# Attention in a two-layer trunk: values stationary on two column tiles, probabilities divided before their transposes

## The chip, the core and the metric

The kernel runs on one core of one Trainium2 chip. The metric is the device time of one execution in microseconds (us). The engines of a core are TensorE (PE, matmuls and transposes; its weight loads are shown as PEld), VectorE (DVE), ScalarE (ACT), GpSimd (POOL) and SyncE (SP, which issues DMAs). Each engine takes its instructions in the order in which the program lists them and waits on semaphores for what the others make. SBUF is the memory on the core, PSUM the one that PE writes.

## The reference

A trunk of two layers on 256 tokens of 1024 channels in float32. Each layer projects the tokens to queries, keys, values (8 heads of 64 channels), a recurrent input and a gate. Attention is causal over three patterns of window and dilation; with the bias table built at the start, the three merge into one softmax per head with a bias by distance:

```
s = (q / 8) k^T + bias            # per head, 256 x 256, causal
p = exp(s - max),  Z = sum(p)     # per head and token
O = (p v) / Z                     # 256 tokens x 512 channels
y = [rms_norm(O) * g_attn, rms_norm(gelu(gate) * h) * g_lru]     # h: linear recurrence
x = layer_norm(alpha x + y W_out)
```

Then comes a feed-forward part: a dense SwiGLU in layer 0, eight SwiGLU experts of which each token takes two in layer 1. RMS norm divides by the root of the mean square over all 512 channels of a token.

## The kernel before

All work is written out in program order, and each engine runs its list from first to last. Products in float32 are made from splits: a matrix is written as a high part (`hi`, by ACT) and the rest (`lo`, by DVE, as the difference), and three matmuls hi*hi, hi*lo, lo*hi replace one. Weights come in units of 1 MB through a stream of buffers (`WeightStream`): a DMA is issued when a buffer becomes free, which is when the split that reads it is done. `U.ahead(n)` puts the splits of the next units into the lists of ACT and DVE at that place. The list of what may be loaded ends early until the router has told which experts come (`U.open`); after that the expert stage streams all remaining weights. Experts with at most 64 tokens work on unsplit weights in two column tiles: 64 stationary columns go to output partitions 0 to 63, 64 others to 64 to 127.

In a mixer the order around the change is this. PE projects keys, gate and values. Scores get bias and maximum on DVE, and ACT takes the exponentials into `P0[par]` (queries 0 to 127: 128 tokens x 4 heads x 128 keys) and `P1[par]` (queries 128 to 255, 256 keys), one pair for the even heads and one for the odd, with the sums in `Z` (token x half x head). After the projection of the values (`vt`) PE transposes the probabilities (L719 to L723), four 128x128 blocks at a time: eight blocks of each parity into a PSUM buffer `big`, four into a buffer `sm`. ACT copies the eight to `PTa` (L724), DVE the four to `PTb` (L725). There are two `big` buffers, and the next user of both is the recurrent branch's part of the output product. ACT then squares the branch's result `gt` (L726), POOL adds the squares over the four channel blocks (L727, L728), and the output product of the recurrent branch runs on PE in two calls of `out_l` of 24 matmuls each. Between the two stand the sum of the squares over the partitions by a matmul with ones (`pss`), from which DVE and POOL make the factor `rl` (L361, L362), and probabilities times values: 8 matmuls for the first 128 queries, 16 for the others, with the transposed probabilities as stationary and 64 channels of one head as moving operand. The result has tokens on partitions. DVE multiplies it by 1/Z (L777), ACT squares and sums it (L778), DVE and POOL make `ra`, PE transposes it in blocks (L785, four inside the second `out_l`, four behind), and ACT and DVE split the transposes into `Ah` and `Al` (L792, L794). With these runs the attention part of the output product, 48 matmuls, whose results are added to the residual with the factor `ra` (L820).

The listing gives the code with its line numbers; in the profile nearly all matmuls carry L245, the line of the helper.

Of the kernel before, what the change touches and what calls it, by code (L numbers as in the profile page):

```python
# [9 lines left out]
F32 = mybir.dt.float32  # L10
F32R = mybir.dt.float32r
I32 = mybir.dt.int32
AF = mybir.ActivationFunctionType
ALU = mybir.AluOpType
AX = mybir.AxisListType

P = 128
D = 1024
S = 256
H = 8  # L20
DA = 512
# [7 lines left out]
RMS_EPS = 1e-6  # L29
# [174 lines left out]
def trunk(ctx, tc, x, xT, w_in, w_out, prm, wbd, rb, ohc, cst, ln1_g, ln1_b, ln2_g, ln2_b,  # L204
          ffn_w_gate, ffn_w_up, ffn_w_down, router_w, moe_w_gate, moe_w_up, moe_w_down, out):
    nc = tc.nc
    V, A, T, G = nc.vector, nc.scalar, nc.tensor, nc.gpsimd
# [8 lines left out]
    def sm(shape=None):  # L216
        cnt[0] += 1
        t = ps.tile([P, 512], F32, name=f"sm{cnt[0]}", tag="sm", bufs=4)
        if shape:
            t = t.rearrange("p (a b) -> p a b", a=shape)  # L220
        return t
# [22 lines left out]
    def mm(o, l, r, first, last):  # L244
        T.matmul(o, l, r, start=first, stop=last)  # L245

    units = []
    TS = [slice(0, P), slice(P, S)]
# [79 lines left out]
    ident = csts[:, 0:128]  # L328
# [12 lines left out]
    ones = base.tile([P, 2], F32, name="ones")  # L341
# [18 lines left out]
    def rsqrt(o, ms, eps, scale):  # L360
        V.tensor_scalar(o, ms, scale, eps, op0=ALU.mult, op1=ALU.add)  # L361
        G.tensor_tensor(out=o, in0=o, in1=mhalf, op=ALU.pow)  # L362
# [194 lines left out]
    def mixer(L, pool, prev):  # L557
        def mt(shape, name, dt=F32):
            if name in SLOT:
                return pool.tile(shape, dt, name=f"{name}_{L}", tag=f"m4_{SLOT[name]}")  # L560
            m2 = math.prod(shape[1:]) == 512
            if m2:
                return pool.tile(shape, dt, name=f"{name}_{L}", tag="m2", bufs=NM2)
            return lnp.tile(shape, dt, name=f"{name}_{L}", tag=name)
# [22 lines left out]
        if prev is None:  # L587
            banks()
            p = big(2)
# [29 lines left out]
        for g, (dst, bi) in enumerate(((rg, 5), (ig, 6))):  # L619
            p = big(4)  # L620
# [31 lines left out]
        P0 = [mt([P, 4, P], f"P0{par}") for par in range(2)]  # L652
# [59 lines left out]
        PTb = [mt([P, 4, P], f"PTb{par}") for par in range(2)]  # L712
        A.activation(Lh, gt, AF.Copy)
        V.tensor_tensor(out=Ll, in0=gt, in1=Lh.bitcast(F32), op=ALU.subtract)
        for par in range(2):
            pa = big(8)
            pb = sm(4)
            for c in range(4):
                T.transpose(pa[:, c, :], P0[par][:, c, :], ident)  # L719
            for c in range(4):  # L720
                T.transpose(pa[:, 4 + c, :], P1[par][:, c, 0:P], ident)
            for c in range(4):
                T.transpose(pb[:, c, :], P1[par][:, c, P:S], ident)  # L723
            A.activation(PTa[par].rearrange("p j c q -> p (j c) q"), pa, AF.Copy)  # L724
            V.tensor_copy(PTb[par], pb)  # L725
        A.activation(tg, gt, AF.Square)  # L726
        G.tensor_tensor(out=tg[:, 0:2], in0=tg[:, 0:2], in1=tg[:, 2:4], op=ALU.add)  # L727
        G.tensor_tensor(out=tg[:, 0], in0=tg[:, 0], in1=tg[:, 1], op=ALU.add)  # L728
        V.reciprocal(Z, Z)

        r = [ax[:, t, :] for t in range(2)]

# [2 lines left out]
        def out_l(u, mid=None):  # L735
            wh, wl = U.next(2)
            for t in range(2):
                if t and mid:
                    mid()
                if u == 0:  # L740
                    pl[t] = big(2)
                p = pl[t]
                for j in range(2):
                    c = 2 * u + j
                    down_mm((p[:, 0, :], p[:, 1, :]), c == 0, c == 3, Lh[:, c, TS[t]], Ll[:, c, TS[t]],
                            wh[:, j, :], wl[:, j, :])

        def out_r(t):
            V.scalar_tensor_tensor(r[t], pl[t].rearrange("p a b -> p (a b)"), rl[:, t:t + 1], r[t],
                                   op0=ALU.mult, op1=ALU.add)  # L750
# [10 lines left out]
        U.ahead(4)  # L761
        Ah = mt([P, 4, S], "Ah", F32R)
        Al = mt([P, 4, S], "Al", F32R)
        O = mt([P, 2, H, 64], "O")
        Of = [O[:, t].rearrange("p h c -> p (h c)") for t in range(2)]
        for t in range(2):
            sq = mt([P, DA], f"sq{t}")
            p = sm(8)
            for h in range(H):
                par, c = h % 2, h // 2  # L770
                hv = slice(h * 64, (h + 1) * 64)
                if t == 0:
                    mm(p[:, h, :], PTa[par][:, 0, c, :], vt[:, 0, hv], True, True)
                else:
                    mm(p[:, h, :], PTa[par][:, 1, c, :], vt[:, 0, hv], True, False)
                    mm(p[:, h, :], PTb[par][:, c, :], vt[:, 1, hv], False, True)
            V.tensor_tensor(out=O[:, t], in0=p, in1=Z[:, t, :, None].to_broadcast([P, H, 64]), op=ALU.mult)  # L777
            A.activation(sq, Of[t], AF.Square, accum_out=ra[:, t:t + 1])  # L778
            rsqrt(ra[:, t:t + 1], ra[:, t:t + 1], RMS_EPS, 1.0 / DA)
        oT = []  # L780

        def o_transposes(t):
            q = sm(4)
            for c in range(4):
                T.transpose(q[:, c, :], Of[t][:, c * P:(c + 1) * P], ident)  # L785
            oT.append(q)

        out_l(1, lambda: o_transposes(0))
        o_transposes(1)
        for t in range(2):  # L790
            q = oT[t]
            A.activation(Ah[:, :, TS[t]], q, AF.Copy)  # L792
            out_r(t)
            V.tensor_tensor(out=Al[:, :, TS[t]], in0=q, in1=Ah[:, :, TS[t]].bitcast(F32), op=ALU.subtract)  # L794

        if L < DEPTH - 1:
            U._lo(G)
# [692 lines left out]
```

## Time and profile before

| | us |
|---|---|
| median of 3 runs (1257.7 to 1260.06) | 1258.46 |
| the profiled execution | 1258.07 |
| its span, first to last instruction | 1256.2 |
| PE busy in the span | 1214.9 (97%) |
| DVE busy | 650.0 (52%) |
| ACT busy | 518.1 (41%) |
| POOL busy | 81.7 (7%) |
| mean DMA rate | 341 GB/s |

Times in the rows are microseconds from the span's start. A row of a timeline gives the start, the duration from the start of the first to the end of the last of its instructions, the engine, the line, the operation, output and inputs by name (buffer numbers left out), partitions x elements, the count, and in brackets how long the engine stood idle before and what released it. Layer 0's mixer comes first (the rows of it lie between 74 and 96 us), then the dense part (its splits L833 run from 127.1 to 286.9), then layer 1's mixer (its rows lie between 365 and 386 us), the router, and the expert stage, which takes the rest.

### The profile page before, as it was taken

How to read it: one execution, taken by the hardware profiler on the slowest of the kernel's cores; microseconds unless marked ns; L12 is line 12 of the kernel's file. 1: busy time of each engine (PE TensorE's matmuls, PEld its weight loads, DVE VectorE, ACT ScalarE, POOL GpSimd, SP SyncE). 2: the span in 40 equal slices, each digit the busy share in tenths (PEclk: the TensorE clock that was granted, in tenths of full speed). 3: DMA queues.
4: the chain of work that ended last, by engine and by line, in shares of the span. 5: the costliest groups of instructions: out<-in, count | busy, mean ns of one | idle time of the engine just before them, and what ended most of it. 6: DMA issues, size and time to landing. Idle time of an engine off the chain costs nothing. (4 is left out here: it accounts for less than half of the span.)

```text
span 1256.2 us, 18532 instructions
## 1 busy us (share of the span) xinstructions
PE 1214.9 (97%) x7562; PEld 908.3 (72%) x7562; DVE 650.0 (52%) x611; ACT 518.1 (41%) x549; POOL 81.7 (7%) x75
## 2 busy tenths in 40 slices
PE   9999999999999989999999999999999999999884
PEld 8989999998988766666655678875568887565441
DVE  6698544457698964544310398841069883101004
ACT  5784533343782742444210377731057772000001
POOL 3224000004014010000000000000000000000001
PEclk9999999999999999999999999999999999999998
DMA  9853545553468959999999999999999999999993
GB/s 348 317 194 137 200 193 202 201 193 145 158 247 348 373 230 369 420 421 420 421 419 420 420 421 421 421 420 420 421 420 421 421 421 418 421 420 420 421 418 144
DMA packets 63506, 428.99 MB, mean 341 GB/s; under 512 B 7951, under 2 KB 8376, under 8 KB 12984
## 3 DMA queue, kind: packets, MB, share of 16 engines
q1 hardware_dynamic: 62408, 423.55, 83.0%
q0 software_dynamic: 720, 3.68, 0.8%
q8 instruction: 61, 1.00, 0.3%
q10 hardware_dynamic: 288, 0.52, 0.1%
q14 instruction: 29, 0.24, 0.1%
HBM read 426.67 MB, written 2.63 MB: 342 GB/s over the span
## 5 line engine op out<-in xcount | busy, mean ns | idle before, releaser
L148 DVE TENSOR_TENSOR lo<-w,hi 128x2048 fp32r<-128x2048 f32 (+1 forms) x181 | 402.8, 2242 | 79.9 <-ACT hi L130 78.2
L130 ACT ACTIVATE hi<-w 128x2048 fp32r<-128x2048 f32 (+1 forms) x183 | 340.7, 1875 | 88.2 <-PE sm L245 43.9
L245 PE MATMUL sm<-w,g 128*64 128x256 f32 x2240 | 260.9, 382 | 1.4 <-DMA w<-in_moe_w_up_dram 0.9
L245 PEld LDWEIGHTS sm<-w,g 128*64 128x64 f32 x2240 | 157.7, 137 | 95.3 <-issue 23.7
L245 PE MATMUL sm<-hi,g 128*128 128x512 f32 x672 | 220.3, 399 | 0.1
L1280 DVE TENSOR_TENSOR h<-h,sm 128x256 f32<-128x256 f32 (+1 forms) x56 | 29.0, 518 | 273.9 <-PE sm L245 273.9
L1176 ACT ACTIVATE ht<-sm 128x256 f32<-128x256 f32 (+1 forms) x56 | 25.6, 457 | 311.5 <-PE sm L1174 311.5
L245 PEld LDWEIGHTS sm<-hi,g 128*128 128x128 f32 x672 | 126.2, 188 | 32.1 <-issue 2.4
L245 PE MATMUL acc<-w,ht 128*64 128x512 f32 x560 | 135.0, 602 | 10.4 <-DMA w<-in_moe_w_down_dram 9.9
L245 PE MATMUL sm<-lo,g 128*128 128x512 f32 x336 | 133.1, 396 | 1.9 <-DVE lo L148 1.9
L245 PE MATMUL sm<-xh,hi 128*128 128x256 f32 x528 | 132.4, 284 | 0.0
L245 PE MATMUL sm<-xl,hi 128*128 128x256 f32 x528 | 131.9, 283 | 0.0
L245 PE MATMUL acc<-hi,ht 128*128 128x512 f32 x336 | 111.5, 403 | 0.0
L245 PEld LDWEIGHTS sm<-xh,hi 128*128 128x128 f32 x528 | 99.8, 189 | 1.7 <-issue 1.3
L245 PEld LDWEIGHTS acc<-w,ht 128*64 128x64 f32 x560 | 40.3, 138 | 83.4 <-issue 67.6
L245 PEld LDWEIGHTS sm<-xl,hi 128*128 128x128 f32 x528 | 99.6, 189 | 0.4
L245 PE MATMUL sm<-xh,lo 128*128 128x256 f32 x528 | 84.8, 283 | 0.0
L245 PEld LDWEIGHTS acc<-hi,ht 128*128 128x128 f32 x336 | 64.3, 191 | 17.5 <-issue 2.7
L245 PE MATMUL acc<-lo,ht 128*128 128x512 f32 x168 | 68.1, 406 | 8.6 <-DVE lo L148 8.6
L245 PEld LDWEIGHTS sm<-lo,g 128*128 128x128 f32 x336 | 63.2, 188 | 16.8 <-DVE lo L148 2.9
L245 PEld LDWEIGHTS sm<-xh,lo 128*128 128x128 f32 x528 | 72.2, 189 | 0.0
L362 POOL TENSOR_TENSOR mv<-mv,mhalf 128x1 f32<-128x1 f32 x8 | 7.0, 876 | 788.4 <-DVE mv L361 788.4
(260 smaller groups left out, 1174.0 us busy)
## 6 DMA issues: line engine op xcount, KB each, us to landing
w<-in_moe_w_gate_dram SPq DMA_DIRECT2D x112, 1024.0 KB, 19.8
w<-in_moe_w_up_dram SPq DMA_DIRECT2D x112, 1024.0 KB, 19.7
w<-in_moe_w_down_dram SPq DMA_DIRECT2D x110, 1024.0 KB, 19.7
w<-in_w_in_dram SPq DMA_DIRECT2D x18, 1024.0 KB, 6.3
w<-in_ffn_w_gate_dram SPq DMA_DIRECT2D x11, 1024.0 KB, 4.8
w<-in_ffn_w_up_dram SPq DMA_DIRECT2D x11, 1024.0 KB, 5.3
w<-in_ffn_w_down_dram SPq DMA_DIRECT2D x11, 1024.0 KB, 6.1
w<-in_w_out_dram SPq DMA_DIRECT2D x8, 1024.0 KB, 4.9
```

The costliest lines, as they stand in the source:

```text
L130: self.nc.scalar.activation(hi[a], w[a], AF.Copy)
L148: V.tensor_tensor(out=lo[a], in0=w[a], in1=hi[a].bitcast(F32), op=ALU.subtract)
L245: T.matmul(o, l, r, start=first, stop=last)
L362: G.tensor_tensor(out=o, in0=o, in1=mhalf, op=ALU.pow)
L1176: A.activation(ht[0], p[:, 0:nj, :], AF.Copy)
L1280: V.tensor_tensor(out=h, in0=h, in1=pu, op=ALU.mult)
```

## The change

The softmax sums are used earlier: 1/Z is taken ahead of the transposes, and DVE multiplies the four tiles of probabilities by it in place. Probabilities times values changes its sides: 64 channels of one head are the stationary operand, the transposed probabilities move (256 queries for the first 128 keys, 128 queries for the last 128), the even head of a pair goes to output partitions 0 to 63 and the odd one to 64 to 127. So the result has channels on partitions, as the output product wants it: there is no product with 1/Z behind it and no transpose. ACT writes `Ah` straight from it and then its squares (into a tile called O), DVE writes `Al`, POOL adds the squares over the channel blocks, and PE sums them over the partitions with ones (`psq`), behind the second `out_l`.

```diff
--- before.py
+++ after.py
@@ -712,6 +712,12 @@
         PTb = [mt([P, 4, P], f"PTb{par}") for par in range(2)]
         A.activation(Lh, gt, AF.Copy)
         V.tensor_tensor(out=Ll, in0=gt, in1=Lh.bitcast(F32), op=ALU.subtract)
+        V.reciprocal(Z, Z)
+        Zv = Z.rearrange("p t (c a) -> p t a c", a=2)
+        for par in range(2):
+            for t, Pt in enumerate((P0[par], P1[par])):
+                V.tensor_tensor(out=Pt, in0=Pt, in1=Zv[:, t, par, :, None].to_broadcast([P, 4, (t + 1) * P]),
+                                op=ALU.mult)
         for par in range(2):
             pa = big(8)
             pb = sm(4)
@@ -726,7 +732,6 @@
         A.activation(tg, gt, AF.Square)
         G.tensor_tensor(out=tg[:, 0:2], in0=tg[:, 0:2], in1=tg[:, 2:4], op=ALU.add)
         G.tensor_tensor(out=tg[:, 0], in0=tg[:, 0], in1=tg[:, 1], op=ALU.add)
-        V.reciprocal(Z, Z)
 
         r = [ax[:, t, :] for t in range(2)]
 
@@ -761,37 +766,34 @@
         U.ahead(4)
         Ah = mt([P, 4, S], "Ah", F32R)
         Al = mt([P, 4, S], "Al", F32R)
-        O = mt([P, 2, H, 64], "O")
-        Of = [O[:, t].rearrange("p h c -> p (h c)") for t in range(2)]
+        sq = mt([P, 4, S], "O")
+        po = [sm(2), sm(2)]
+        for c in range(4):
+            for kt, q in ((0, slice(0, S)), (1, slice(P, S))):
+                for par in range(2):
+                    rows = slice(par * 64, par * 64 + 64)
+                    h = 2 * c + par
+                    pt = PTb[par][:, c, :] if kt else PTa[par][:, :, c, :]
+                    mm(po[c // 2][rows, c % 2, q], vt[:, kt, h * 64:h * 64 + 64], pt, kt == 0, kt == 1)
+        for j in range(2):
+            o = slice(2 * j, 2 * j + 2)
+            A.activation(Ah[:, o, :], po[j], AF.Copy)
+            V.tensor_tensor(out=Al[:, o, :], in0=po[j], in1=Ah[:, o, :].bitcast(F32), op=ALU.subtract)
+            A.activation(sq[:, o, :], po[j], AF.Square)
+        G.tensor_tensor(out=sq[:, 0:2], in0=sq[:, 0:2], in1=sq[:, 2:4], op=ALU.add)
+        G.tensor_tensor(out=sq[:, 0], in0=sq[:, 0], in1=sq[:, 1], op=ALU.add)
+        out_l(1)
         for t in range(2):
-            sq = mt([P, DA], f"sq{t}")
-            p = sm(8)
-            for h in range(H):
-                par, c = h % 2, h // 2
-                hv = slice(h * 64, (h + 1) * 64)
-                if t == 0:
-                    mm(p[:, h, :], PTa[par][:, 0, c, :], vt[:, 0, hv], True, True)
-                else:
-                    mm(p[:, h, :], PTa[par][:, 1, c, :], vt[:, 0, hv], True, False)
-                    mm(p[:, h, :], PTb[par][:, c, :], vt[:, 1, hv], False, True)
-            V.tensor_tensor(out=O[:, t], in0=p, in1=Z[:, t, :, None].to_broadcast([P, H, 64]), op=ALU.mult)
-            A.activation(sq, Of[t], AF.Square, accum_out=ra[:, t:t + 1])
-            rsqrt(ra[:, t:t + 1], ra[:, t:t + 1], RMS_EPS, 1.0 / DA)
-        oT = []
-
-        def o_transposes(t):
-            q = sm(4)
-            for c in range(4):
-                T.transpose(q[:, c, :], Of[t][:, c * P:(c + 1) * P], ident)
-            oT.append(q)
-
-        out_l(1, lambda: o_transposes(0))
-        o_transposes(1)
-        for t in range(2):
-            q = oT[t]
-            A.activation(Ah[:, :, TS[t]], q, AF.Copy)
             out_r(t)
-            V.tensor_tensor(out=Al[:, :, TS[t]], in0=q, in1=Ah[:, :, TS[t]].bitcast(F32), op=ALU.subtract)
+        psq = sm()
+
+        def norm_o():
+            for t in range(2):
+                mm(psq[:, t * 2:t * 2 + 2], sq[:, 0, TS[t]], ones, True, True)
+            for t in range(2):
+                rsqrt(ra[:, t:t + 1], psq[:, t * 2:t * 2 + 1], RMS_EPS, 1.0 / DA)
+
+        norm_o()
 
         if L < DEPTH - 1:
             U._lo(G)
```

The new products stand on DVE between the split of the recurrent branch (`Ll`) and the copies of PTb. Before, DVE's order in layer 0:

```order
L714 TENSOR_TENSOR Ll_864<-gt_631,Lh_863 128x1024
L725 COPY PTb_0_869<-sm_874 128x512
L725 COPY PTb_0_870<-sm_890 128x512
L729 RECIPROCAL Z_695<-Z_695 128x16
L753 TENSOR_SCALAR ax<-ax 128x2048
```

After, at the same place (P_0_690 and P_0_692 are P0 and P1 of the even heads, P_0_691 and P_0_693 of the odd):

```order
L714 TENSOR_TENSOR Ll_864<-gt_631,Lh_863 128x1024
L715 RECIPROCAL Z_695<-Z_695 128x16
L719 TENSOR_TENSOR P_0_690<-P_0_690,Z_695 128x512
L719 TENSOR_TENSOR P_0_692<-P_0_692,Z_695 128x1024
L719 TENSOR_TENSOR P_0_691<-P_0_691,Z_695 128x512
L719 TENSOR_TENSOR P_0_693<-P_0_693,Z_695 128x1024
L731 COPY PTb_0_869<-sm_879 128x512
```

Four products and the reciprocal now come ahead of the copies; on PE the transposes keep their place behind the projection of the values.

The second place is POOL's list in layer 0 from the squares of the recurrent branch (tg) on. Before:

```order
L727 TENSOR_TENSOR tg_632<-tg_632 128x512
L728 TENSOR_TENSOR tg_632<-tg_632 128x256
L362 TENSOR_TENSOR rl_865<-rl_865,mhalf 128x1 x2
L362 TENSOR_TENSOR ra_866<-ra_866,mhalf 128x1 x2
L148 TENSOR_TENSOR lo_1054<-w_859,hi_1052 128x2048
```

After, where O_979 is the tile of the squares of attention:

```order
L733 TENSOR_TENSOR tg_632<-tg_632 128x512
L734 TENSOR_TENSOR tg_632<-tg_632 128x256
L362 TENSOR_TENSOR rl_865<-rl_865,mhalf 128x1 x2
L783 TENSOR_TENSOR O_979<-O_979 128x512
L784 TENSOR_TENSOR O_979<-O_979 128x256
L362 TENSOR_TENSOR ra_866<-ra_866,mhalf 128x1 x2
```

The two additions stand between the powers for rl and those for ra.

The third place is PE in layer 0, the end of the second `out_l` and the start of the attention part. Before:

```order
L245 MATMUL big_939<-hi_910,Ll_864 128x512 x2
L785 MATMUL sm_1041<-csts,O_975 128x128 x4
L245 MATMUL sm_1062<-hi_918,Ah_973 128x512
L245 MATMUL sm_1062<-lo_921,Ah_973 128x512
L245 MATMUL sm_1062<-hi_918,Ah_973 128x512
```

After:

```order
L245 MATMUL big_943<-hi_914,Ll_864 128x512 x2
L245 MATMUL sm_1032<-ones,O_979 128x2 x2
L245 MATMUL sm_1049<-hi_922,Ah_977 128x512
L245 MATMUL sm_1049<-lo_925,Ah_977 128x512
L245 MATMUL sm_1049<-hi_922,Ah_977 128x512
```

The transposes of O have gone, and two matmuls that read the squares stand in their place.

## Rows read from the trace of the kernel before

**Rows 1.** The page: engine, busy us, share of the span, instructions.
```profile
PE 1214.9 (97%) x7562; PEld 908.3 (72%) x7562; DVE 650.0 (52%) x611; ACT 518.1 (41%) x549; POOL 81.7 (7%) x75
```

**Rows 2.** Stretches: busy us by engine (instructions), granted clock, DMA share, GB/s.
```profile
456.00:462.00 6.00, 6.00 (x38) 4.05 (x36) 0.00 (x0) 0.00 (x0) 0.00 (x0) 1.00 0.03 11
...
470.00:476.00 6.00, 3.91 (x9) 3.14 (x10) 4.57 (x3) 0.00 (x0) 0.00 (x0) 0.50 0.44 160
476.00:478.00 2.00, 2.00 (x8) 1.56 (x8) 0.00 (x0) 0.00 (x0) 0.00 (x0) 0.82 1.07 451
...
502.00:1236.00 734.00, 716.29 (x4298) 467.61 (x4298) 307.73 (x239) 253.15 (x227) 0.00 (x0) 1.00 1.01 418
```

**Rows 3.** Timeline of PE, layer 0.
```profile
74.90 0.60 PE L719 MATMUL big<-csts,P 128*128 128x128 f32 x4
...
77.08 0.60 PE L723 MATMUL sm<-csts,P 128*128 128x128 f32 x4
77.61 0.50 PE L245 MATMUL big<-hi,Lh 128*128 128x512 f32 x1
...
83.34 0.61 PE L245 MATMUL sm<-ones,tg 128*128 128x2 f32 x4
83.81 2.20 PE L245 MATMUL sm<-vt,PTa 128*128 128x64 f32 x18
...
89.17 0.48 PE L245 MATMUL big<-hi,Lh 128*128 128x512 f32 x1
...
95.76 0.48 PE L245 MATMUL sm<-hi,Ah 128*128 128x512 f32 x1
```

**Rows 4.** Timeline of DVE, layer 0.
```profile
76.80 1.22 DVE L714 TENSOR_TENSOR Ll<-gt,Lh 128x1024 fp32r<-128x1024 f32 x1
77.93 1.28 DVE L725 COPY PTb<-sm 128x512 f32<-128x512 f32 x2
79.13 0.24 DVE L729 RECIPROCAL Z<-Z 128x16 f32<-128x16 f32 x1
...
89.21 2.28 DVE L148 TENSOR_TENSOR lo<-w,hi 128x2048 fp32r<-128x2048 f32 x1
91.41 0.68 DVE L777 TENSOR_TENSOR O<-sm,Z 128x512 f32<-128x512 f32 x1
```

**Rows 5.** Timeline of ACT, layer 0.
```profile
78.35 1.07 ACT L726 ACTIVATE tg<-gt 128x1024 f32<-128x1024 f32 x1
```

**Rows 6.** Timeline of POOL, layer 0, then layer 1.
```profile
79.50 2.11 POOL L727 TENSOR_TENSOR tg<-tg 128x512 f32<-128x512 f32 x1 [26.65 <-ACT tg L726]
81.69 1.60 POOL L728 TENSOR_TENSOR tg<-tg 128x256 f32<-128x256 f32 x1
86.92 4.99 POOL L362 TENSOR_TENSOR rl<-rl,mhalf 128x1 f32<-128x1 f32 x2 [3.62 <-DVE rl L361]
93.11 0.55 POOL L362 TENSOR_TENSOR ra<-ra,mhalf 128x1 f32<-128x1 f32 x1 [1.21 <-DVE ra L361]
...
369.71 1.30 POOL L727 TENSOR_TENSOR tg<-tg 128x512 f32<-128x512 f32 x1 [63.37 <-ACT tg L726]
...
376.31 4.98 POOL L362 TENSOR_TENSOR rl<-rl,mhalf 128x1 f32<-128x1 f32 x2 [3.62 <-DVE rl L361]
```

**Rows 7.** Timeline of layer 1, three engines.
```profile
365.11 0.60 PE L719 MATMUL big<-csts,P 128*128 128x128 f32 x4
...
367.48 1.22 DVE L714 TENSOR_TENSOR Ll<-gt,Lh 128x1024 fp32r<-128x1024 f32 x1
...
368.56 1.07 ACT L726 ACTIVATE tg<-gt 128x1024 f32<-128x1024 f32 x1
...
385.56 0.47 PE L245 MATMUL sm<-hi,Ah 128*128 128x512 f32 x1
```

**Rows 8.** Timeline of PE, expert stage: column tiles, and a wait.
```profile
461.96 5.40 PE L245 MATMUL sm<-w,g 128*64 128x256 f32 x48
...
472.09 0.79 PE L245 MATMUL acc<-lo,ht 128*128 128x512 f32 x1 [4.29 <-DVE lo L148]
```

## The prediction

> **What bounds the kernel now.** The page comes first: TensorE (PE) is busy 97% of the span [rows 1], so whatever leaves PE without work makes the kernel longer, unless a later stage gives the time back. Whether one does is read from the table by stretches [rows 2]. From 502 us to 1236 us the DMA share is 1.01: there the stream of expert weights sets the pace. But from 456 to 462 us the same stream stands still (share 0.03), and from 470 to 476 us it is at 0.44: before 502 us it waits for buffers that PE, ScalarE (ACT) and VectorE (DVE) have to empty. The long full stretch thus begins at a time that the mixers, which lie before it, set. I therefore count what a mixer loses or gains at PE one to one at the end.
>
> Then the timelines of the two mixers. In layer 0 the transposes of the probabilities (L719 to L723) follow on the projection of the values without a gap at 74.90, their last four begin at 77.08, and the recurrent branch's part of the output product (48 matmuls into `big`) begins its first 24 at 77.61; the small matmuls that sum the branch's squares stand at 83.34, probabilities times values from 83.81 to 89.17, the other 24 from there on, and the attention part of the output product begins at 95.76 [rows 3]. DVE at that time has no air: it ends the low half `Ll` at 78.02 (76.80 + 1.22), and it does the copies of PTb, the reciprocal, and later the split L148 (89.21 to 91.49) right before the product L777, which begins at 91.41 [rows 4]. So DVE, not PE, already sets when O is ready. ACT squares the recurrent branch at 78.35 [rows 5], and GpSimd (POOL) adds those squares and takes the powers for rl, which end at 91.91 [rows 6]. Layer 1 has the same picture [rows 7].
>
> **The change part by part.** All moments are those of the profiled execution, whose own time is 1258.07 us over a span of 1256.2 us.
>
> *The four products P times 1/Z, ahead of the transposes.* The order puts the reciprocal and four products (128x512, 128x1024, 128x512, 128x1024) on DVE behind `Ll`, and the transposes on PE read what they write. The reciprocal takes 0.24, a 512 product with Z spread along the row 0.68 (L777, the same operation on as many elements), a 1024 one 1.22 (L714); each starts some 0.09 before the one ahead of it is over (77.93 against 78.02) [rows 4]. From 77.93 on: reciprocal to 78.2, products done at about 78.9, 80.0, 80.6 and 81.8. PE wanted the first at 74.90. Four transposes take 0.436 (five groups of four from 74.90 to 77.08) [rows 3], so with the last eight starting at 81.85 they would be over at 82.7 instead of 77.5: **+5.2 us**. Nothing hides this: PE works in order, behind the transposes wait all matmuls of the mixer, and the output product also needs the `big` buffers that the copies PTa empty.
>
> *The clock.* PE has nothing to do from 74.90 to 78.95, 4.05 us. [...] I take this row as the price: four transposes then last 0.87. They run 78.95 to 79.8, from 80.05 (second product) to 81.8, and, never waiting again, to 82.7 and 84.45; the eight that fill the second `big` are over at 83.55 instead of about 82.25. Lower bound for this term: nothing.
>
> *What follows on ACT, DVE and POOL.* PTa of the odd heads can be copied from 83.65, and the square that follows it on ACT begins at about 84.55 instead of 78.35: **+6.2 us**. The chain behind it keeps its order: high halves of the output weights, their low halves on DVE, rl, two more low halves, L148, and on POOL the two powers, which end 0.42 after L148 (91.91 against 91.49) [rows 4, 6]. It moves as a whole, so the powers end at 98.1. In layer 0 it may come up to 0.8 nearer, if the first POOL addition, 2.11 there, takes 1.30 as in layer 1 [rows 6].
>
> *Probabilities times values.* 24 matmuls (two machine instructions each) of 128 weights and 64 moving columns took 5.36 (83.81 to 89.17) [rows 3]. Now there are 16 matmuls: 16 instructions with 256 moving columns and 16 with 128, on two halves of the columns. The expert stage has the 256 form: 48 in 5.40, 0.1125 each [rows 8]. So 1.8 for these; for those with 128 between half of it and the whole, 0.9 to 1.8, and I take 1.05 since the moving side halves. Sum 2.85, a gain of 2.5. The upper bound is no gain at all, 5.36, if the halves don't run beside each other with this operand. The eight transposes of O go (0.9), and so do L777, L778 and their rsqrt between PE and Ah.
>
> *The new sum of squares.* ACT writes Ah and the squares directly from the results (four passes over 512 columns, while PE does the rest of the recurrent branch's product), DVE writes Al; neither is late. But the squares are now added by POOL, in 512 and 256 columns, and POOL's queue holds the two rl powers ahead of them. They start at 98.1. The 512 addition took 1.30 in layer 1 and 2.11 in layer 0, the 256 one 1.60 beside DVE's low halves [rows 6]. I take 1.30, and half of that, 0.65, for the 256 one, because DVE then runs Al and the residual additions, each with one operand from PSUM, and not the low halves: 1.95, with 3.71 as the upper bound. Ready at 100.1. PE's four small matmuls take 0.47 (83.34 to 83.81), and the attention part of the output product begins at 100.6 instead of 95.76: **layer 0 +4.9 us**. PE itself would be there earlier: 84.45, plus 5.5 for the first 24 matmuls into `big` (77.61 to 83.34 less a short wait, 0.23 each [rows 3]), 0.5, 2.85 and 5.5 for the next 24 is 98.8. So it waits some 1.3 us, and the gain on the values lies in that wait. The powers for ra (0.55 each [rows 6]) are over before the first addition to the residual wants them, 2.75 us of matmuls later.
>
> [...]
>
> *Layer 1.* `Ll` ends at 368.70, so the products end at about 372.5; PE idles from 365.11 to 369.6, 4.5 us, and the clock falls as above. At half clock the second `big` is full at 374.3, PTa follows, and the square begins at 375.35 instead of 368.56, +6.8 [rows 7]. Powers at 381.29 + 6.8 = 388.1 [rows 6], additions 390.0, output product 390.5 against 385.56 [rows 7]: **+5.0 us**.
>
> Sum: 1258.07 + 4.9 + 5.0 = 1268.0 us. The profiled execution lies 0.4 under the median of the runs (1258.46), which is within what the sum can tell.
>
> **The rivals.**
> *The clock stays at full speed.* The two waits are broken off by transposes, and the row for the fall is a single one. Then the chain moves by 4.9 in layer 0 and 5.45 in layer 1 instead of 6.2 and 6.8, and the layers lose 3.5 and 3.65: 1265.2 us. Against it: each wait is about as long as the one in the row.
>
> *PE, not POOL, ends last.* If the two halves of the columns don't run beside each other (5.36 instead of 2.85), PE reaches the small matmuls at 101.4 in layer 0 and 392.0 in layer 1, and the losses are 6.2 and 6.9: 1271.2 us. If the clock stays low through the first 24 matmuls into `big` (24 matmuls at twice 0.23, 5.5 more), while the halves do run side by side, they are 9.1 and 9.9: 1277.1 us. Contended additions on POOL give 1271.5. For it: each needs only one of my choices to be wrong. Against it: the expert stage shows the halves side by side.
>
> *The weight stream takes the loss back.* In 502 to 1236 us it alone sets the end. If it could use layer 1's stall to load ahead, that layer would cost nothing: 1263.0 us; with the gains of PE, about 1260. Against it: its pauses at 456 and 470 us show it out of buffers, not out of time [rows 2].
>
> *Faster: the products are hidden.* Place: DVE ahead of the transposes. Price: without the wait each layer keeps 2.5 + 0.9 - 0.47 = 2.9 us, so 1252.2 us. It decides at the moment when DVE starts the products: up to about 71.4 in layer 0 they would all be done when PE wants them. DVE is then still at the gate branch and does the low half of a weight and `Ll` to 78.02, 6.6 us too late, and its order is fixed.
>
> **How the numbers follow.** The forecast 62%, full clock 12%, PE or POOL later 19%, the stream 4%, hidden products 3%. The predicted time is 1268 us. The range reaches from full clock with the 0.8 and a short POOL (1263.5) to the cases where one of PE's terms is at its bound (1273.5); the case of a low clock through those 24 matmuls lies outside. About 0.2% (2.5 us) is what a measurement tells from no change. Faster by more: 3%, the hidden products. Within: 4%, the stream with the gains of PE. Slower by more: 93%.
>
> **What would show it.** In the changed trace PE must stand without work for about 4 us in front of the first transposes of P, released by the products on DVE, in both layers; the granted clock must show 0.50 over the next few microseconds; probabilities times values must take about 2.9 us; and PE must wait some 1 us for POOL ahead of the small matmuls that stand in front of the attention part of the output product. Full DMA share must begin about 10 us later than now. I am wrong if the transposes start at the old time, if the small matmuls find the squares ready, or if the stream's full stretch begins no later than before.

## The result and the profile after

The changed kernel takes 1278.8 us (median of 5 runs, 1277.06 to 1280.97) where the kernel before, run beside it, takes 1259.26 us (5 runs, 1257.7 to 1260.08). The ratio is 1.0156, 95% interval 1.0144 to 1.0168: 19.5 us more. The forecast was 1268.0 with a range to 1273.5. The direction was right, the size was half of what came. The profiled execution has a span of 1275.3 us, 19.1 more than before, and PE is still busy 96% (97% before [rows 1]).

First PE in layer 0, from the changed kernel's timeline: start, duration, engine, line, operation, count, and in brackets the idle time before and what ended it. L725 to L729 are the transposes of the probabilities.

```profile
74.37 0.39 PE L245 MATMUL sm<-hi,xl 128*128 128x512 f32 x1
...
78.71 0.63 PE L725 MATMUL big<-csts,P 128*128 128x128 f32 x4 [3.95 <-issue]
...
79.80 1.11 PE L727 MATMUL big<-csts,P 128*128 128x128 f32 x4 [0.47 <-DVE P L719]
...
89.57 0.65 PE L245 MATMUL sm<-PTa,vt 128*64 128x256 f32 x4
...
92.00 0.39 PE L245 MATMUL sm<-PTb,vt 128*64 128x128 f32 x4
...
101.98 1.01 PE L245 MATMUL sm<-ones,O 128*128 128x2 f32 x4 [3.89 <-POOL O L784]
...
102.85 0.77 PE L245 MATMUL sm<-hi,Ah 128*128 128x512 f32 x1
```

The transposes began at 78.71 instead of 74.90, and the attention part of the output product (`hi,Ah`) at 102.85 instead of 95.76 [rows 3]: 7.1 us later, where 4.9 were forecast. There are two waits of about 4 us, and the forecast had only the first. (What released the first reads `issue` in layer 0; layer 1's row below names the products, L719.) Probabilities times values took 2.75 us (89.57 to about 92.32), 5.36 before [rows 3].

The same kernel's stretches, in the columns of [rows 2], show a fall of the clock behind each wait:

```profile
80.00:83.00 3.00, 3.00 (x15) 3.00 (x15) 2.17 (x3) 1.03 (x1) 0.00 (x0) 0.50 0.25 104
...
96.00:98.00 2.00, 2.00 (x10) 1.38 (x8) 1.29 (x2) 0.67 (x2) 1.11 (x1) 1.00 0.98 397
...
102.00:107.00 5.00, 5.00 (x14) 4.13 (x15) 0.23 (x2) 0.00 (x0) 3.73 (x3) 0.50 0.15 62
107.00:108.00 1.00, 1.00 (x6) 0.82 (x5) 0.12 (x1) 0.00 (x0) 1.00 (x1) 1.00 0.00 0
```

After the second wait the first five microseconds of the attention part ran at a granted clock of 0.50, 14 instructions in 5 us. Layer 1 repeats the picture:

```profile
378.74 1.09 PE L725 MATMUL big<-csts,P 128*128 128x128 f32 x4 [4.36 <-DVE P L719]
...
402.00 1.02 PE L245 MATMUL sm<-ones,O 128*128 128x2 f32 x4 [3.73 <-POOL O L784]
...
402.88 0.77 PE L245 MATMUL sm<-hi,Ah 128*128 128x512 f32 x1
```

From these rows the loss can be booked. PE came to layer 1's first wait at 378.74 - 4.36 = 374.38, where it began at 365.11 before [rows 7]: 9.3 us were lost by then, 7.1 up to 102.85 and 2.2 in the slow stretch behind it. `hi,Ah` of layer 1 began at 402.88 against 385.56 [rows 7], 17.3 us, so 8.0 of it in layer 1. The end is 19.1 late. The remaining 1.8 is about what the second slow stretch costs (402 to 407 is at 0.50 as well): the last matmuls of layer 1's attention part begin 12.8 us behind its first (415.70), where it was 10.7 before (396.30). So the loss passed through to the end about one to one, as forecast. What was wrong lies inside the mixers: 9.3 and 9.8 instead of 4.9 and 5.0.

What made the second wait stands in ACT's list and in DVE's. ACT, changed kernel, layer 0: L780 writes Ah, L782 the squares (into O).

```profile
93.30 0.58 ACT L780 ACTIVATE Ah<-sm 128x512 fp32r<-128x512 f32 x1
97.33 0.60 ACT L782 ACTIVATE O<-sm 128x512 f32<-128x512 f32 x1 [3.45 <-DVE Al L781]
97.82 0.59 ACT L780 ACTIVATE Ah<-sm 128x512 fp32r<-128x512 f32 x1
99.17 0.60 ACT L782 ACTIVATE O<-sm 128x512 f32<-128x512 f32 x1 [0.76 <-DVE Al L781]
```

DVE of the same kernel at the same time; L148 is the split of a later weight, L781 writes Al:

```profile
94.41 2.28 DVE L148 TENSOR_TENSOR lo<-w,hi 128x2048 fp32r<-128x2048 f32 x1
96.62 0.68 DVE L781 TENSOR_TENSOR Al<-sm,Ah 128x512 fp32r<-128x512 f32 x1
98.44 0.69 DVE L781 TENSOR_TENSOR Al<-sm,Ah 128x512 fp32r<-128x512 f32 x1 [1.15 <-ACT Ah L780]
```

And POOL of the same kernel: the powers for rl (L362), then the additions of the squares.

```profile
92.12 4.99 POOL L362 TENSOR_TENSOR rl<-rl,mhalf 128x1 f32<-128x1 f32 x2 [3.62 <-DVE rl L361]
99.84 1.28 POOL L783 TENSOR_TENSOR O<-O 128x512 f32<-128x512 f32 x1 [2.74 <-ACT O L782]
101.20 0.73 POOL L784 TENSOR_TENSOR O<-O 128x256 f32<-128x256 f32 x1
```

Layer 1 repeats this too (waits of 3.37 us on ACT and 2.74 us on POOL). The square could have followed Ah at 93.8. It reads nothing that Al writes, yet it waited 3.45 us for Al, which stood behind L148. What the two share is the tile `po[j]` in PSUM that both read. The second Ah stands behind the first square, the second Al behind the second Ah, the second square behind that Al. POOL had ended the powers at 97.11, a little earlier than the forecast's 98.1, and then waited 2.74 us for the last square.

### The profile page after: what moved, and what is told of

The parts are those of the page before. It is cut to its first block, busy times and chain, and to the rows that moved or that the text cites. A ratio compares the mean times of both kernels' runs of the same rounds, so it can differ in the third digit from the quotient of the medians.

```text
span 1275.3 us, 18466 instructions
## 1 busy us (share of the span) xinstructions
PE 1218.0 (96%) x7522; PEld 908.7 (71%) x7522; DVE 654.0 (51%) x615; ACT 517.7 (41%) x545; POOL 85.2 (7%) x79
## 5 line engine op out<-in xcount | busy, mean ns | idle before, releaser
L148 DVE TENSOR_TENSOR lo<-w,hi 128x2048 fp32r<-128x2048 f32 (+1 forms) x181 | 402.5, 2242 | 79.5 <-ACT hi L130 78.3
L245 PEld LDWEIGHTS acc<-w,ht 128*64 128x64 f32 x560 | 40.4, 138 | 81.8 <-issue 66.1
L362 POOL TENSOR_TENSOR mv<-mv,mhalf 128x1 f32<-128x1 f32 x8 | 7.0, 878 | 791.0 <-DVE mv L361 791.0
```

Of the source, the lines that this page charges most:

```text
L148: V.tensor_tensor(out=lo[a], in0=w[a], in1=hi[a].bitcast(F32), op=ALU.subtract)
```

## The experiments

The theory after this reading: the surplus is one line of ACT's list, a square that is held by another reader of the same PSUM tile, and the clock's fall that the longer wait draws after it. Ratios below are to the kernel before in the runs beside it (medians 1259.26, 1260.47, 1260.48 and 1260.89 in four groups of runs), with their 95% intervals.

| kernel | us (range, runs) | ratio |
|---|---|---|
| changed | 1278.8 (1277.06 to 1280.97, 5) | 1.0156 [1.0144, 1.0168] |
| square ahead of Al | 1268.2 (1267.44 to 1272.19, 4) | 1.0074 [1.0046, 1.0103] |
| square reads Ah | 1271.13 (1270.14 to 1271.9, 4) | 1.0086 [1.0065, 1.0107] |
| no division | 1268.42 (1266.97 to 1270.82, 4) | 1.0067 [1.0040, 1.0094] |
| square ahead, no division | 1256.82 (1255.2 to 1261.26, 10) | 0.9969 [0.9956, 0.9983] |
| square ahead, PE kept busy | 1267.2 (1264.14 to 1268.5, 5) | 1.0061 [1.0042, 1.0080] |
| square ahead, sums late | 1269.15 (1267.76 to 1269.56, 4) | 1.0066 [1.0045, 1.0087] |
| square ahead, early divisions | 1265.44 (1263.8 to 1267.34, 7) | 1.0043 [1.0028, 1.0058] |
| early divisions, sums late | 1262.35 (1258.96 to 1265.43, 12) | 1.0018 [1.0005, 1.0031] |
| the same, copy first | 1263.73 (1262.26 to 1266.18, 12) | 1.0023 [1.0013, 1.0033] |
| square ahead, no division, sums late | 1253.12 (1250.95 to 1256.42, 6) | 0.9947 [0.9931, 0.9962] |

Moments of two profiles can't be set against each other as they stand: in four of the profiles (square reads Ah; square ahead, no division; square ahead, early divisions; copy first; not in those of the kernel before and the changed one) DVE waits 1.98 to 2.72 us for the DMA of the bias table at about 60 us, and what follows in layer 0 comes later. So a profile is also measured here from the last matmul of layer 0's projection of the values (74.37 in the first row of the changed kernel above) to the same one in layer 1. That took 290.2 us in the kernel before and 299.6 in the changed one, 9.4 more.

**The square ahead of Al.** One line moves:

```diff
             A.activation(Ah[:, o, :], po[j], AF.Copy)
+            A.activation(sq[:, o, :], po[j], AF.Square)
             V.tensor_tensor(out=Al[:, o, :], in0=po[j], in1=Ah[:, o, :].bitcast(F32), op=ALU.subtract)
-            A.activation(sq[:, o, :], po[j], AF.Square)
```

Expected: 

> The changed kernel with one line moved: ACT's square stands ahead of DVE's Al in the program, so that ACT's list (Ah, square, Ah, square) is not broken by a reader of the same PSUM tile on another engine. My theory: in the changed kernel the first square waited for Al because both read one PSUM bank and the order between the two readers is kept by a semaphore, and Al stood behind L148; this made POOL's additions late, PE's second wait 3.9 us instead of 1.2, and that wait cost a second fall of the clock. Then here the squares are done by about 95.6, POOL starts when the powers for rl end (97.1), PE's second wait is about 1.2 us, the granted clock stays at 1.00 there, and each layer gains 3.2 + 2.0 = 5.2 us: 1278.8 - 10.4 = 1268.4 us. Rival A: the square waited for something else that DVE does before (the split L148, by way of a buffer): no change, 1278.8. Rival B: the wait gets shorter but the clock falls all the same: 1278.8 - 6.4 = 1272.4.

Measured 1268.2, where the theory had 1268.4. PE, layer 0 and layer 1:

```profile
79.12 1.09 PE L725 MATMUL big<-csts,P 128*128 128x128 f32 x4 [3.96 <-issue]
...
99.86 0.61 PE L245 MATMUL sm<-ones,O 128*128 128x2 f32 x4 [1.13 <-POOL O L784]
...
394.14 0.61 PE L245 MATMUL sm<-ones,O 128*128 128x2 f32 x4 [1.05 <-POOL O L784]
```

PE's second wait is 1.13 and 1.05 us, and the stretch behind it is at full clock:

```profile
102.00:107.00 5.00, 5.00 (x23) 4.12 (x22) 2.30 (x4) 0.00 (x0) 4.73 (x2) 1.00 0.08 30
```

23 instructions where the changed kernel's same stretch had 14. That is the prediction's picture: it had PE waiting 1.3 us there and the attention part beginning at 100.6; it began at 100.33. So the place of this line is worth some 10.6 us (medians of two groups of runs).

**Is it the shared tile?** Moving the line also changes ACT's order. Here the order stays (Ah, Al, square), and the square reads Ah from SBUF; its squares are those of the rounded values.

```diff
-            A.activation(sq[:, o, :], po[j], AF.Square)
+            A.activation(sq[:, o, :], Ah[:, o, :].bitcast(F32), AF.Square)
```

Expected: 

> The changed kernel with its order kept (Ah, Al, square), but the square reads Ah, the copy in SBUF that ACT has just written, and not the PSUM tile po. (The squares are then those of the rounded values.) Theory (square and Al read the same PSUM tile and are put one behind the other, so the square waits for Al, which is queued on DVE): with nothing shared the 3.45 us wait of the first square goes as it did when the square stood ahead of Al, PE's wait for the sums falls from 3.9 to about 1.1 us, and the time is that of the kernel with the square first, 1268.2 us (1266.5 to 1270). Rival (it is the place in ACT's row or DVE's load that makes the square late, not the shared tile): nothing moves, 1278.8. Second rival (the wait stays but only the second clock fall goes): about 1274.

ACT of this kernel, layer 0:

```profile
94.78 0.58 ACT L780 ACTIVATE Ah<-sm 128x512 fp32r<-128x512 f32 x1
95.39 0.63 ACT L782 ACTIVATE O<-Ah 128x512 f32<-128x512 f32 x1
95.93 0.58 ACT L780 ACTIVATE Ah<-sm 128x512 fp32r<-128x512 f32 x1
96.54 0.63 ACT L782 ACTIVATE O<-Ah 128x512 f32<-128x512 f32 x1
```

and DVE:

```profile
98.09 1.27 DVE L781 TENSOR_TENSOR Al<-sm,Ah 128x512 fp32r<-128x512 f32 x2
```

The wait of 3.45 us is gone with order and neighbours unchanged, and DVE wrote both Al in one go at 98.09, later than all squares. So the tile that both read is the cause, and neither the place in the list nor DVE's load alone. PE waited 1.14 and 0.53 us for the sums, and behind both waits the `Ah` matmuls begin 0.23 us apart (0.42 in the changed kernel's stretch at 0.50). The time, 1271.13, is 2.9 above the kernel with the line moved and over the forecast band's 1270. The intervals overlap, and this profile is one of those with a late start (1.98 us for the bias table). From the projection of the values to that of layer 1 the two kernels take the same, 294.4 (75.97 to 370.39) and 294.8 us (74.78 to 369.54). What the rest is, behind that, stays open.

So two reads of one tile stood one behind the other here, at a price of 3.45 us. What put them in that order, and whether a bank of PSUM has a part in it, as the expectation for the square ahead of Al had it, no trace shows.

**No division.** The reciprocal stays, the four products go; the result is then not normalised.

```diff
-            for t, Pt in enumerate((P0[par], P1[par])):
-                V.tensor_tensor(out=Pt, in0=Pt, in1=Zv[...].to_broadcast([...]), op=ALU.mult)
```

Expected, with the square where the change has it: 

> The changed kernel without the four products of the probabilities with 1/Z: the division by the softmax sums is left out. It prices PE's first wait, the fall of the clock behind it included. My theory: the transposes start at about 74.6 again, the first wait and its fall of the clock go, the chain from the square of the recurrent branch on comes earlier by 6.2 us in layer 0 and about 6.5 in layer 1, and the second wait stays as it is, with its own fall of the clock: 1278.8 - 12.7 = 1266.1 us. Rival: the second wait is bound by something that does not move with the transposes, so that PE, which comes earlier, waits longer there: a gain of less than half, above 1272.

and with the square moved as well: 

> Both edits together: the square ahead of Al, and no products with 1/Z (the division by the softmax sums is left out). If the two losses stand apart, they add: 1278.8 - 10.4 - 12.7 = 1255.7 us, 3.6 under the kernel before, which would be what the column tiles and the missing transposes of O give. If POOL's additions behind the rl powers still bind, PE waits some 2 us for them and the gain over before is about 1 us per layer: 1257. Rival: above 1262, then a third loss is in the change that neither edit takes out.

Without the products the transposes began at once (75.56 in layer 0), and the whole time came out at 1268.42, 2.3 over the theory; PE now waited 4.92 and 3.77 us for the squares, since it reached that place sooner. With both, 1256.82: below the kernel before with the whole interval, and at the theory's second number, 1257. What PE still waits for the sums is 1.61 and 1.00 us (PE, layers 0 and 1; the profile is that of the slowest of the ten runs, 1261.26):

```profile
97.12 0.61 PE L245 MATMUL sm<-ones,O 128*128 128x2 f32 x4 [1.61 <-POOL O L780]
...
386.88 0.61 PE L245 MATMUL sm<-ones,O 128*128 128x2 f32 x4 [1.00 <-POOL O L780]
```

So the divisions in front of the transposes cost 1268.2 - 1256.8 = 11.4 us (10.4 where the square is held, 1278.8 - 1268.4), the held square 10.6, and the layout itself gains 3.6 (1260.47, the kernel before beside it, less 1256.82): 18.4 by these medians of two groups, against 19.5 measured in one.

**PE kept busy.** To price the first fall of the clock, 15 matmuls of constants into the `big` buffer stand in front of the first transposes.

```diff
-            pa = big(8)
+            pf = big()
+            if par == 0:
+                keep_warm(15, pf)
+            pa = pf.rearrange("p (a b) -> p a b", a=8)
```

Expected: 

> The first of these kernels (square ahead of Al) with 15 matmuls on constants (512 columns, 0.23 us each, 3.4 us) in front of the first transposes of the probabilities, in both layers: they fill PE's first wait and write into the buffer that the transposes then overwrite. It prices the fall of the clock at that wait alone. My theory: the granted clock stays at 1.00, the eight transposes that fill the second buffer are done 1.2 us earlier, and since ACT, DVE and POOL hang on them, the layer gains as much: 1268.4 - 2.4 = 1266.0 us. Rival: the clock costs nothing there, since the products on DVE release the last transposes anyway: 1268.4.

The clock did what was wanted, here over the waits of both layers:

```profile
78.00:80.00 2.00, 0.92 (x6) 0.46 (x5) 1.97 (x4) 0.00 (x0) 0.00 (x0) 1.00 0.81 307
80.00:82.00 2.00, 1.70 (x14) 1.49 (x15) 2.00 (x3) 1.03 (x1) 0.00 (x0) 1.00 0.44 184
...
370.00:384.00 14.00, 12.34 (x78) 9.90 (x78) 11.41 (x13) 8.73 (x9) 2.91 (x2) 1.00 0.54 220
```

By the timelines layer 1's sums of squares came at 392.06 instead of 394.14, 2.1 us earlier. Of these 0.4 were there before the first wait (PE's last matmul ahead of it began at 74.39 instead of 74.78). Counted from that matmul the sums came 1.2 us earlier in layer 0 and 0.5 in layer 1, where the forecast had 1.3 to 1.4 a layer. By the runs it is 1.0 in all, between the theory (1266.0) and the rival (1268.4), and the intervals lie over each other: what the first fall is worth in the whole time is not resolved.

**Can the divisions be hidden?** In the kernel before, POOL does nothing between 60 us and the addition at 79.50 [rows 6], and the sums of the even heads are ready at about 64. So the even heads' products go to POOL right behind the scores' maxima; the odd ones are shared by DVE (small) and POOL (large) behind `tg*gt`.

```diff
+        inverse(0)
+        product(G, 0, 0)
+        product(G, 0, 1)
...
         V.tensor_tensor(out=tg, in0=tg, in1=gt, op=ALU.mult)
+        inverse(1)
+        product(V, 1, 0)
+        product(G, 1, 1)
```

Expected: 

> The kernel with the square first, and the divisions moved: the even heads' reciprocals come right behind the scores' maxima and POOL, idle there, makes their two products at about 65 to 70 us; the odd heads' reciprocals come behind tg*gt on DVE, the small odd product on DVE and the large one on POOL, about 71.5 to 75. Theory: all are done before PE ends the V product at 74.4 (even) and reaches the odd transposes at 76.7, the 4.0 and 4.4 us waits go and the clock does not fall: the time of the kernel that has neither the wait nor the division, 1256.8 (1255 to 1259). Rival: POOL beside DVE takes twice as long (the larger product 3 to 5 us) and slows DVE's two-input operations, so that PE waits 1 to 3 us per layer without a clock fall: 1259 to 1263.

Measured 1265.44: the theory's 1256.8 is missed by far and even the rival's 1263 by 2.4. The products were out of the way in time; what they displaced shows in layer 1 (layer 0 of this profile started late). POOL, then DVE:

```profile
360.76 4.94 POOL L690 TENSOR_TENSOR P<-P,Zr 128x512 f32<-128x512 f32 x2 [50.43 <-DVE Zr L686]
367.76 2.35 POOL L690 TENSOR_TENSOR P<-P,Zr 128x1024 f32<-128x1024 f32 x1 [2.06 <-PE sm L245]
```

```profile
361.25 2.70 DVE L148 TENSOR_TENSOR lo<-w,hi 128x2048 fp32r<-128x2048 f32 x1 [0.64 <-ACT hi L130]
363.87 2.38 DVE L701 TENSOR_SCALAR tg<-tg 128x1024 f32<-128x1024 f32 x1
...
368.70 2.49 DVE L707 SCALAR_TENSOR_TENSOR gt<-tg,gt 128x1024 f32<-128x1024 f32 x1 [0.35 <-ACT tg L706]
...
374.75 1.22 DVE L729 TENSOR_TENSOR Ll<-gt,Lh 128x1024 fp32r<-128x1024 f32 x1
```

In the kernel before, beside an idle POOL, DVE had taken 0.69 and 1.23 us for the two instructions at the same place:

```profile
359.48 0.69 DVE L689 TENSOR_SCALAR tg<-tg 128x1024 f32<-128x1024 f32 x1
...
362.69 1.23 DVE L692 SCALAR_TENSOR_TENSOR gt<-tg,gt 128x1024 f32<-128x1024 f32 x1 [1.27 <-ACT tg L691]
```

Here each ended some 0.5 to 1.1 us behind a POOL product (about 365.7 and 370.1) and took 2.38 and 2.49. By these rows POOL's products cost DVE time. `gt`, Lh and Ll came later, and PE waited behind the transposes instead of ahead of them, this time for 2.27 us (PE, layer 1):

```profile
374.50 0.50 PE L245 MATMUL big<-hi,Lh 128*128 128x512 f32 x1 [2.27 <-ACT PTa L739]
```

The stretches of this kernel show the clock at 0.50 behind that:

```profile
377.00:379.00 2.00, 2.00 (x6) 1.58 (x5) 1.79 (x3) 2.00 (x3) 1.92 (x2) 0.50 0.99 410
```

That is the rival's mechanism, with the fall of the clock that it had left out; how long POOL's products take without DVE beside them no run shows. The 8.6 us above the kernel without the division are not booked beyond that.

The first POOL group ended at 365.70 and the TENSOR_SCALAR, 2.38 us for 0.69, came 0.55 us later. What holds the one beside the other, these rows do not show. POOL's times differ beside a TENSOR_SCALAR too: layer 0 of the kernel before, and the same two instructions of the changed kernel:

```profile
79.29 1.17 DVE L753 TENSOR_SCALAR ax<-ax 128x2048 f32<-128x2048 f32 x1
...
84.43 1.22 DVE L758 TENSOR_SCALAR ax<-ax 128x2048 f32<-128x2048 f32 x1
85.45 1.36 POOL L733 TENSOR_TENSOR tg<-tg 128x512 f32<-128x512 f32 x1 [33.12 <-ACT tg L732]
```

In the kernel before POOL's addition began at 79.50, inside the TENSOR_SCALAR, and took 2.11 us [rows 6]; in the changed kernel it began 0.2 us before the TENSOR_SCALAR's end and took 1.36. Both ended some 1.15 us behind the TENSOR_SCALAR.

**The sums late.** PE's four small matmuls on the squares move behind the first 8 matmuls of the attention part.

```diff
-        norm_o()
...
+            if t == 0 and hf == 0:
+                m.insert(8, norm_o)
```

Expected, with the square moved alone: 

> The kernel with the square first, and the sums of squares of the attention part (4 matmuls with a column of ones) issued behind the first 8 matmuls of the output product instead of ahead of it; the POOL subtraction of a weight that followed the powers follows them still. Theory: PE waited 1.13 and 1.05 us for POOL's adds at that place and this goes, since 8 matmuls (about 2 us at the full clock) now stand ahead: 1268.2 - 2.2 = 1266.0. Rival: the out product's first scaled add on DVE now waits for the powers (up to 4.99 us, issued about 2 us later) and its PSUM buffers come free late, so that PE waits for a buffer instead: 1268 to 1270.

with the early divisions too: 

> The early divisions and the late sums of squares together. Theory: the two gains add, 1256.8 - 2.2 = 1254.6 (1253 to 1257), which is below the kernel before (1260). Rival: the remaining waits are hidden behind the weights that come in and nothing is gained over the early divisions alone, 1256.8.

and, as the bound of the layout, with no division at all: 

> The bound that the new layout could reach with free divisions: square first, sums of squares late, and no division of the probabilities at all (the result is not normalised). Theory: 1256.8 (square first and no division) less the waits of 1.61 and 1.00 us that remained there = 1254.3 (1252.5 to 1256). If so, the fewer and shorter matmuls of the new layout are worth some 6 us of 1260, and the divisions alone turn it into a loss. Rival: the waits left there are hidden by what comes next and nothing goes: 1256.8.

The wait of about 1 us for the sums is gone in all three. Alone the edit isn't told from nothing (1269.15 where 1268.2 were had without it; ratios 1.0066 and 1.0074). The time lies in the rival's band, but its mechanism doesn't show: PE waits for no buffer between 100 and 108 us. From the projection of the values to that of layer 1 this kernel takes 294.5 us, 0.2 less than without the edit, so in layer 0 the wait that went gave hardly anything back. With the early divisions the edit brought 3.1 us, to 1262.35, still 0.18% over the kernel before. The theory (1254.6) and the rival (1256.8) both fail there, since both took 1256.8 for the early divisions. Without divisions 1253.12, in the theory's range, PE without any wait over 0.35 us between 70 and 110: the layout could be worth 0.5% if the divisions were free.

**Copy first.** In the version with early divisions and late sums PE waits 2.26 us a layer for the copy PTa, which stands behind Lh on ACT. Here the even heads' copies are issued ahead of Lh and Ll.

```diff
-        A.activation(Lh, gt, AF.Copy)
-        V.tensor_tensor(out=Ll, in0=gt, in1=Lh.bitcast(F32), op=ALU.subtract)
         for par in range(2):
...
             V.tensor_copy(PTb[par], pb)
+            if par == 0:
+                A.activation(Lh, gt, AF.Copy)
+                V.tensor_tensor(out=Ll, in0=gt, in1=Lh.bitcast(F32), op=ALU.subtract)
```

Expected: 

> The kernel with the early divisions and the late sums of squares, and ACT's copy of the even heads' transposes (PTa) and DVE's (PTb) issued ahead of Lh and Ll instead of behind them. Before it, PE's first product of the local part waited 2.26 us in each layer for that copy, which stood behind Lh (78.12 to 79.18) and so ended at 80.05. Theory: the copy ends before Lh can start (gt is ready at 78.1), PE then waits for Lh alone, until about 79.3: 0.9 us less in each layer, 1262.4 - 1.8 = 1260.6 (1259 to 1262), equal to the kernel before within the interval. Rival: Ll, which stands behind a weight subtraction and the PTb copy on DVE, ends later by 0.7 us and PE waits there instead: 1261.5 to 1263.

The rival's mechanism came true, and the time, 1263.73, lies 0.7 above its range. PE, layer 1, where the version without this edit waited 2.25 us for PTa and 0.34 for Ll:

```profile
374.46 0.50 PE L245 MATMUL big<-hi,Lh 128*128 128x512 f32 x1 [1.39 <-ACT Lh L743]
...
377.46 1.22 PE L245 MATMUL big<-hi,Ll 128*128 128x512 f32 x2 [1.80 <-DVE Ll L744]
```

2.59 us of waiting became 3.19 in layer 1; in layer 0 the same two waits went from 2.59 to 1.86. DVE ends last here: Ll, late by what DVE takes longer beside POOL's products (layer 0: L148, the TENSOR_SCALAR and the SCALAR_TENSOR_TENSOR took 3.06, 2.38 and 2.48 us, in the kernel before 2.29, 0.69 and 1.23). By the times the two versions are not told apart (ratios 1.0018 and 1.0023, intervals overlapping). No version with the division beat the kernel before.

## Why the prediction was wrong

**The step that failed** stands under the new sum of squares: "ACT writes Ah and the squares directly from the results (...), DVE writes Al; neither is late." The squares and Al were both late. I had followed each engine's queue but only the data between engines: Al needs Ah, the squares need nothing of Al. That ACT's square would stand behind DVE's Al, with which it shares only the PSUM tile that both read, was not in the working, and Al stood behind a split of 2.28 us on DVE. Measured: 3.45 us of wait on ACT, 2.74 on POOL beyond the powers, and the attention part 2.25 us later than forecast in layer 0 (102.85 for 100.6, although the powers had ended 1 us sooner than forecast).

**Its second cost** was not in the sum either: PE's wait there became 3.89 instead of 1.3 us, and behind it the clock fell once more (0.50 from 102 to 107 us): 2.2 us in layer 0 and about 1.8 to 2.1 in layer 1. The same price, which I had taken for the first wait from [rows 8], should have been put on every wait that a late edge could stretch to 4 us. Both layers together: 9.3 - 4.9 = 4.4 and 9.8 - 5.0 = 4.8, so 9.2 us of surplus. The version with that line moved came out at the forecast (1268.2; 1268.0). As a loss it is 10.0 us between the two profiled spans (1266.2 and 1256.2), where 9.9 were forecast; by the medians of the runs it is 7.7, since the kernel before, beside it, had 1260.47.

**What held.** The four products (77.92 to 81.49; the forecast's end was 81.8), the wait of about 4 us in front of the transposes and the clock at 0.50 behind it (four transposes took 0.85 us, 80.71 to 81.56, where the working put 0.87, twice the 0.436 of [rows 3], by the 0.50 of [rows 2] around the wait of [rows 8]), the branch's square on ACT (84.31 for 84.55), probabilities times values (2.75 for 2.85), the additions on POOL (1.28 and 0.73 for 1.30 and 0.65), and the loss passing through the expert stage whole.

**The rivals.** "PE, not POOL, ends last" and its 1271 to 1277 did not happen by its mechanism: POOL ended last, only later. That the clock stays up was false at the transposes (0.50 from 80 to 83 us). The stream took nothing back. That it alone sets the end from 502 us on is not shown either: in the same row PE is busy 716.29 of 734 us [rows 2]. Hidden products were run in one placement, on POOL and DVE ahead of the transposes, and they don't hide there: the price was given as 1252.2, which the kernel without any division nearly reaches (1253.12), but with early products DVE took 2.38 and 2.49 us where it had taken 0.69 and 1.23. Other placements, on ACT for one, were not run.

**Additions beside VectorE.** The working put POOL's second addition at 0.65 us, half of the first, on the ground that the DVE instructions beside it have one operand from PSUM; no run shows that the place of an operand decides it. What the runs show is the times. Beside the residual additions (L754) in the changed kernel, and beside Al and them with the square ahead, the two took 1.28 and 0.73 us. The branch's addition of 256 columns, beside the low halves (L150), took 1.61 us in the changed kernel (86.89). And the 2.11 us of [rows 6], which went into the upper bound, stood beside the TENSOR_SCALAR at 79.29 shown above.

## What to carry to other kernels

When a result in PSUM gets a second reader on another engine, allow for the second read standing behind the first, in the order listed, as it did here (3.45 and 3.37 us of wait), and ask what is queued ahead of the first on its engine; issue the reader with the free engine first, or let it read the copy in SBUF (both took the wait away here). A wait of about 4 us on a busy TensorE must be priced with the slow stretch behind it (0.50 in layer 0 and 0.50 to 0.55 in layer 1 of the changed kernel, 0.50 behind the 4.92 and 3.77 us without the division), and a step that lengthens a short wait into such a one costs that again. Idle time on POOL was not free time here (DVE beside its products took 2.38 us for 0.69): count what DVE runs beside it.

## What the runs showed that was not expected

- Two product instructions of POOL on 128x512 and 128x1024 (4.94 us together) stretched DVE's one-input TENSOR_SCALAR from 0.69 to 2.38 us and L148 from about 2.28 to 2.70 and 3.06; a third (2.35 us) stretched the two-input SCALAR_TENSOR_TENSOR from 1.23 to 2.49, a smaller factor than that of the TENSOR_SCALAR.
- Waits shorter than the 4 us of the forecast were followed by either clock. Waits of 1.0 to 1.1 us were not followed by a low one (1.00 behind them), but 1.61 us in the kernel with the square ahead and no division was. In the kernel with early divisions and late sums, 2.26 us and then 0.33 in layer 0 left the clock at 1.00, and 2.25 us and then 0.34 in layer 1 did not. So the length of a wait alone doesn't tell which clock comes behind it. The three stretches in this order:

```profile
100.00:102.00 2.00, 2.00 (x6) 1.59 (x5) 0.00 (x0) 0.00 (x0) 2.00 (x1) 0.51 0.00 0
80.00:84.00 4.00, 3.53 (x14) 2.61 (x15) 4.00 (x5) 4.00 (x6) 1.89 (x2) 1.00 0.58 201
372.00:375.00 3.00, 2.67 (x8) 2.05 (x8) 2.79 (x4) 3.00 (x4) 2.10 (x2) 0.67 0.92 355
```
